# Turning q and k of the attention heads with VectorE and DMA instead of TensorE

## The chip, the cores and the metric

One Trainium2 chip, one core of it. The metric is the device time of one execution in microseconds (us), as a median over several runs; lower is better.

## The reference

One layer of a hybrid encoder over 512 tokens of width 1024, in float32. The normalised input is multiplied by one large matrix, whose columns feed an mLSTM branch (q, k, v, gates i, f, o, z; 4 heads of 256), a stick-breaking attention branch (q, k, v, z; 8 heads of 128) and the merge gates. What the change touches is the attention:

```
h = rmsnorm(x, norm_w);  proj = h @ w_in + b_in
qs = rmsnorm(to_heads(sq, 8), sb_q_norm_w);  ks = rmsnorm(to_heads(sk, 8), sb_k_norm_w)
# per block of 128 queries, for all keys up to its end:
z = (qb @ kb.T) * 128 ** -0.5
log_beta = log_sigmoid(z);  log_1mb = where(s < t, log_sigmoid(-z), 0)
between = reverse_cumsum(log_1mb) - log_1mb
out = where(s < t, exp(log_beta + between), 0) @ v
y_s = out * silu(sz)
...
q, k = silu(causal_depthwise_conv(mq | mk, width 4))        # mLSTM branch
merged = g_m * (y_m @ w_proj_m) + g_s * (y_s @ w_proj_s);  return x + merged @ w_out
```

## The kernel before

Every product is made of three matmuls: each operand is split into a high part (a copy rounded by ScalarE) and a low part (what is left, subtracted by VectorE), and high x high, high x low and low x high are added in PSUM (`mm3`, lines 85 to 87; `split`, lines 90 and 91). In the profile PE is TensorE, DVE VectorE, ACT ScalarE, POOL GpSimd and SP the engine that issues most DMAs.

The program is one list of 118 units, numbered c from 0. A unit is one block of weights and its 24 matmuls of 512 columns. Units 0 to 3 make q, 4 to 7 k, 8 to 11 v and 12 to 15 z of the first set of four attention heads (set 0); 16 to 19 q, 20 to 23 k, 24 to 27 z and 28 to 31 v of the second (set 1). The mLSTM pair 0 follows with o (32 to 35), z (36 to 39), v (40 to 43), q (44 to 47) and k (48 to 51), then pair 1, the gates, the two projections and the last products. The loop at the end of the program runs over the units. In unit c it evacuates unit c-1 from PSUM, splits the weights of unit c+2 (`ahead`; `wh` by ACT, line 90, `wl` by DVE, line 91; the loads on SP, `stg`, line 110, run up to four units ahead), issues the first 12 matmuls, lets each running attention or mLSTM head take one step, and issues the other 12. In the units listed in `REST` running heads take no step, but heads may start. Work that is due later is put off by `defer(n, ...)` to unit c+n, ahead of that unit's split.

A unit of a `tok_group` (q, k, v of the attention, v of the mLSTM) has tokens on the partitions and adds up a quarter of the sum in four banks of PSUM, all evacuated after the fourth. A unit of a `chan_group` has channels on the partitions and is evacuated by itself. The mLSTM's q and k are of that kind: the evacuation is the convolution (lines 646 to 667: a copy by ACT, `acc` in four operations on DVE, a sigmoid on ACT, a product on DVE, then the high part on ACT and the low part on DVE).

An attention head is a generator with a step per unit. Its start (lines 384 to 397) turns q and k of the head, which lie with tokens on partitions (`qraw`, `kraw`), by eight 128x128 transposes on TensorE (line 389) into PSUM and splits them there into `qth`, `qtl`, `kth`, `ktl`; q is scaled by `qkw` on the way. Then come the scores of three blocks and the weighing of two (two sigmoids on ACT, masks on POOL, a scan and a product on DVE, lines 408 to 423), the third block's scores, block transposes of the weights on DVE (line 440), 16 DMAs that finish their turning (line 458), the splits of the turned weights into `ath` and `atl` (lines 467 to 475), and the products with v (line 484), the last followed by the product with the gate into `ys` (line 493). `SB_START` and `M_START` give the first unit in which each head may start; it also waits for its set's k. Sixteen DMAs of 32 KB per mLSTM head turn its output in the same way (lines 780 and 801, `ht` and `hz`).

Of the kernel before, what the change touches and what calls it, by code (L numbers as in the profile page):

```python
# [17 lines left out]
TB = 4  # L18
# [5 lines left out]

SB_START = [10, 13, 16, 19, 26, 28, 31, 34]
M_START = [52, 56, 70, 76]
GATES_PREP, GATES_START = 3, 4
REST = {11, 16, 20, 23, 24, 32, 44, 64}  # L30
AHEAD, LOADS = 2, 4

# [2 lines left out]
def tile_hybrid_layer(  # L35
# [16 lines left out]
    nc = tc.nc  # L52
# [3 lines left out]
    def pool(name, bufs=1, **k):  # L56
# [4 lines left out]
    sp = pool("sp")  # L61
# [4 lines left out]
    ctx.enter_context(tc.manual_schedule())  # L66

    BUFS = {"stg": 3, "wh": 3, "wl": 3, "tmp": 2, "acc": 1, "om": 3, "P5": 2, "A": 4,
            "qk": 18, "vh": 5, "vl": 5, "y": 16, "brow": 1}

    MISC = {"om", "tmp", "acc", "brow", "stg"}

    def blk(tag, dt=F32, shape=(512,), name=None, p=128):

        where = mp if tag in MISC else sp
        return where.tile([p] + list(shape), dt, name=name or tag, tag=tag, bufs=BUFS[tag])

    def dense_ps():
# [111 lines left out]
    def defer(n, fn):  # L190
        later.setdefault(now[0] + n, []).append(fn)
# [19 lines left out]
    ident = cst.tile([128, 128], F32, name="ident")  # L211
# [6 lines left out]
    qkw = cst.tile([128, 1], F32, name="qkw")  # L218
# [91 lines left out]
    done = set()  # L310

    class SbSet:
        def __init__(self, s):
            self.s = s
            self.raw = {"q": [], "k": []}
            self.r = []
            self.v = []

        def z_group(self):
            def evac(ct, ps):  # L320
# [9 lines left out]
        def qk_group(self, name, c0):  # L330
            row = []

            def evac(tb, ps):
                t = blk("qk", name=name + "raw")
                nc.vector.tensor_tensor(t, ps, row[0], op=OP.add)
                self.raw[name].append(t)

                def norm():
                    ssq = tiny.tile([128, 4], F32, name="ssq", bufs=2)
                    rr = tiny.tile([128, 8], F32, name="r" + name, bufs=8 if name == "q" else 4)  # L340
                    r = rr[:, 0:4]
                    junk = blk("acc", BF, (128,), name="sqj")
                    for h in range(4):
                        nc.scalar.activation(junk, t[:, h * 128:(h + 1) * 128], AF.Square,
                                             accum_out=ssq[:, h:h + 1])
                    rstd(r, ssq, 128, EPS)
                    if name == "q":
# [35 lines left out]
        def head(self, h):  # L383
            hs = slice(h * 128, (h + 1) * 128)
            tr = []
            for name in ("q", "k"):
                tp = att_ps()
                for tb in range(TB):
                    nc.tensor.transpose(tp[:, tb * 128:(tb + 1) * 128], self.raw[name][tb][:, hs], ident)  # L389
                th = blk("qk", FR, name=name + "th")  # L390
                tl = blk("qk", FR, name=name + "tl")
                if name == "q":
# [4 lines left out]
                tr.append((th, tl))  # L397
# [218 lines left out]
    class MPair:  # L616
# [25 lines left out]
        def qk_group(self, name, c0, o):  # L642
            def evac(ct, ps):
                ch = o + 4 * self.p + ct
                t = blk("tmp")
                nc.scalar.activation(t, ps, AF.Identity, bias=bias(ch))
                self.prev()
                acc = blk("acc")
                nc.vector.tensor_scalar(acc, t, cw(3, ch), cb(ch), op0=OP.mult, op1=OP.add)
                for j in (1, 2, 3):  # L650
                    nc.vector.scalar_tensor_tensor(acc[:, j:], t[:, 0:T - j], cw(3 - j, ch), acc[:, j:],  # L651
                                                   op0=OP.mult, op1=OP.add)
                self.prev()
                nc.scalar.activation(t, acc, AF.Sigmoid)  # L654

                def mult():
                    nc.vector.scalar_tensor_tensor(t, acc, 1.0 if name == "q" else 0.0625, t,
                                                   op0=OP.mult, op1=OP.mult)

                    def high():  # L660
                        th = blk("qk", FR, name="m%sh" % name)
                        tl = blk("qk", FR, name="m%sl" % name)
                        nc.scalar.activation(th, t, AF.Copy)
                        self.tr[name].append((th, tl))

                        def low():
                            nc.vector.tensor_tensor(tl, t, th.bitcast(F32), op=OP.subtract)
# [12 lines left out]

            chan_group(w_in, c0 + 512 * self.p, 512, h_mov, evac, lambda: self.prev())
# [139 lines left out]
    for p in pairs:  # L821
        p.o_group()
        p.z_group()
        p.v_group()
        p.qk_group("q", C_MQ, 0)
        p.qk_group("k", C_MK, 8)

    gs_t, gm_t = [], []

    def gs_tile(ct):  # L830
        tag = ("brow", "om", "om", "acc", "qk")[min(ct, 4)]
        gs_t.append(blk(tag, shape=(516 if tag == "om" else 512,), name="gs")[:, 0:512])
        return gs_t[ct]

    def gm_tile(ct):
        gm_t.append(blk("qk", name="gm"))
        return gm_t[ct]

    def gate_group(c0, o, tile_of):
# [44 lines left out]
    chan_group(w_proj_s, 0, D, lambda k: ysp[k], ps_evac)  # L884

    merged = []

    def pm_evac(ct, ps):
# [4 lines left out]
        tl = blk("qk", FR, name="mgl")  # L893
# [196 lines left out]

    def first_split(i, low=None):
        u = units[i]
        for j in range(2):
            hi, lo = blk("qk", FR, name="fh"), blk("y", FR, name="fl")
            nc.scalar.activation(hi, u.st[:, j, :], AF.Copy)
            (low or nc.vector).tensor_tensor(lo, u.st[:, j, :], hi.bitcast(F32), op=OP.subtract)  # L1096
            f_w.append((hi, lo))
# [8 lines left out]
    nc.sync.dma_start(gst, w_in[:, C_MI:C_MI + 8].rearrange("(k p) c -> p k c", p=128))  # L1106
    load_vecs()

    idle = blk("qk", FR, name="idle")
    nc.vector.memset(idle.bitcast(F32), 0.0)  # L1110
    wp = dense_ps()

# [137 lines left out]
```

## Time and profile before

| | us |
|---|---|
| median of 3 runs (lowest, highest) | 700.15 (699.52, 700.24) |
| profiled execution, its own time | 700.42 |
| its span | 698.7 |
| TensorE busy | 690.4 |
| VectorE busy | 463.5 |
| ScalarE busy | 335.6 |
| GpSimd busy | 109.2 |

The times in the profile count from the start of the span; what lies around it, 700.42 - 698.7 = 1.7 us, is not in it. A row of a group gives the busy time, the mean duration in ns and the idle time just before; a row of the timeline gives the start, the duration and the instruction, with the idle time before it and what ended it in brackets. A matmul's duration is longer than the distance to the next, since they are pipelined: distances of starts are what counts.

### The profile page before, as it was taken

To read this page: it belongs to the slowest core of one execution; us is meant where nothing else is said; L and a number is where in the kernel's file an instruction comes from. 1 tells how busy PE (TensorE), PEld (TensorE's weight loads), DVE (VectorE), ACT (ScalarE), POOL (GpSimd) and SP (SyncE) were. 2 spreads that over 40 slices of the span, in tenths; PEclk is the share of its full clock that TensorE was granted. 3 is DMA by queue.
4 is the path that set the end of the run, shared out by engine and by line. 5 is a ranking of instruction groups with operands and counts; after the bars stand their busy time and mean duration, and the time that the engine had idled before them with its cause. 6 is when DMAs were issued, how large, how long until landed. Compare 5 with 4: busy or idle time off the path is not lost.

```text
span 698.7 us, 9267 instructions
## 1 busy us (share of the span) xinstructions
PE 690.4 (99%) x3220; PEld 575.2 (82%) x3220; DVE 463.5 (66%) x807; ACT 335.6 (48%) x629; POOL 109.2 (16%) x249
## 2 busy tenths in 40 slices
PE   7999999999999999999999999999999999999997
PEld 5888888888888888888888888888888888888876
DVE  6837887856787775389944738995343364445996
ACT  6245354475554543244475534446563353344451
POOL 5422122252130220000011120001111000111021
PEclk9999999999999999999999999999999999999999
DMA  7432424525433444333332244433323456589434
GB/s 247 136 106 71 126 63 123 148 59 145 112 107 84 130 109 137 90 95 94 97 98 67 61 108 120 120 90 91 91 61 86 112 157 219 144 184 208 126 81 130
DMA packets 104759, 80.94 MB, mean 116 GB/s; under 512 B 6766, under 2 KB 89096, under 8 KB 104712
## 3 DMA queue, kind: packets, MB, share of 16 engines
q1 hardware_dynamic: 102552, 74.45, 37.2%
q0 software_dynamic: 2016, 5.77, 4.5%
q8 instruction: 25, 0.41, 0.2%
q14 instruction: 22, 0.18, 0.1%
q10 hardware_dynamic: 144, 0.13, 0.1%
HBM read 65.12 MB, written 2.10 MB: 96 GB/s over the span
## 4 chain that ended last, share of the span: by engine, by line
PE 97%; DMA 1%; DVE 1%; POOL 0%; SPq 0%; issue 0%; ACT 0%; DVEq 0%
PE dps L85 27%; PE dps L86 27%; PE dps L87 27%; PE aps L86 3%; PE aps L87 3%; PE aps L85 3%; PE aps L389 1%; PE dps L1139 1%; PE dps L1137 1%; PE dps L1138 1%; DMA stg<-in_w_in_dram 1%; PE aps L760 1%; PE aps L762 1%; PE aps L761 1%; DVE fl L1096 0%; POOL fl L1096 0%
## 5 line engine op out<-in xcount | busy, mean ns | idle before, releaser
L91 DVE TENSOR_TENSOR wl<-stg,wh 128x1024 fp32r<-128x1024 f32 x92 | 112.6, 1223 | 112.9 <-ACT wh L90 111.3
L85 PE MATMUL dps<-hh,wh 128*128 128x512 f32 x448 | 175.2, 391 | 0.0
L87 PE MATMUL dps<-hh,wl 128*128 128x512 f32 x448 | 174.5, 389 | 0.0
L86 PE MATMUL dps<-hl,wh 128*128 128x512 f32 x448 | 174.5, 389 | 0.0
L90 ACT ACTIVATE wh<-stg 128x1024 fp32r<-128x1024 f32 x92 | 96.8, 1052 | 58.4 <-PE dps L87 38.2
L87 PEld LDWEIGHTS dps<-hh,wl 128*128 128x128 f32 x448 | 84.1, 188 | 17.8
L85 PEld LDWEIGHTS dps<-hh,wh 128*128 128x128 f32 x448 | 84.1, 188 | 17.1 <-DVE tmp L372 0.4
L86 PEld LDWEIGHTS dps<-hl,wh 128*128 128x128 f32 x448 | 84.2, 188 | 16.9
L85 PE MATMUL dps<-wh,hh 128*128 128x512 f32 x224 | 88.2, 394 | 0.1
L87 PE MATMUL dps<-wh,hl 128*128 128x512 f32 x224 | 87.3, 390 | 0.0
L86 PE MATMUL dps<-wl,hh 128*128 128x512 f32 x224 | 87.3, 390 | 0.0
L87 PEld LDWEIGHTS dps<-wh,hl 128*128 128x128 f32 x224 | 42.0, 188 | 9.0
L85 PEld LDWEIGHTS dps<-wh,hh 128*128 128x128 f32 x224 | 42.1, 188 | 8.6 <-issue 0.5
L86 PEld LDWEIGHTS dps<-wl,hh 128*128 128x128 f32 x224 | 42.1, 188 | 8.1
L651 DVE SCALAR_TENSOR_TENSOR acc<-tmp,vec,acc 128x511 f32<-128x511 f32 (+2 forms) x48 | 36.0, 750 | 1.7
L654 ACT ACTIVATE tmp<-acc 128x512 f32<-128x512 f32 x16 | 10.1, 633 | 50.8 <-DVE acc L651 50.8
L422 DVE TENSOR_TENSOR_SCAN om<-om 128x512 f32<-128x512 f32 (+3 forms) x32 | 26.7, 835 | 8.8 <-POOL om L416 8.8
L416 POOL TENSOR_SCALAR_AFFINE_SELECT om<-om 128x128 f32<-128x128 f32 x32 | 14.1, 441 | 109.0 <-ACT om L414 109.0
L713 POOL TENSOR_SCALAR_AFFINE_SELECT w_all<-om 128x128 f32<-128x128 f32 x16 | 6.0, 412 | 153.9 <-DVE om L708 136.8
L414 ACT ACTIVATE om<-aps,rq 128x512 f32<-128x512 f32 (+3 forms) x32 | 16.8, 525 | 22.8 <-PE aps L87 22.8
L85 PE MATMUL dps<-yh,wh 128*128 128x512 f32 x64 | 24.9, 389 | 0.0
L86 PE MATMUL dps<-yl,wh 128*128 128x512 f32 x64 | 24.9, 389 | 0.0
(271 smaller groups left out, 1225.3 us busy)
## 6 DMA issues: line engine op xcount, KB each, us to landing
stg<-in_w_in_dram SPq DMA_DIRECT2D x87, 512.0 KB, 3.8
az<-ay SPq DMA_DIRECT2D x128, 40.0 KB, 2.0
stg<-in_w_proj_s_dram SPq DMA_DIRECT2D x8, 512.0 KB, 3.7
B<-in_w_out_dram SPq DMA_DIRECT2D x8, 512.0 KB, 4.8
stg<-in_w_proj_m_dram SPq DMA_DIRECT2D x8, 512.0 KB, 3.6
wl<-stg POOLq DMA_DIRECT2D x8, 512.0 KB, 5.5
brow<-in_b_in_dram SPq DMA_DIRECT2D x8, 256.0 KB, 4.0
hz<-ht SPq DMA_DIRECT2D x64, 32.0 KB, 1.9
```

Source lines behind the costliest of these rows:

```text
L85: nc.tensor.matmul(ps, ah, bh, start=first, stop=False)
L86: nc.tensor.matmul(ps, ah, bl, start=False, stop=False)
L87: nc.tensor.matmul(ps, al, bh, start=False, stop=last)
L90: nc.scalar.activation(hi, src, AF.Copy)
L91: nc.vector.tensor_tensor(lo, src, hi.bitcast(F32), op=OP.subtract)
L389: nc.tensor.transpose(tp[:, tb * 128:(tb + 1) * 128], self.raw[name][tb][:, hs], ident)
L414: nc.scalar.activation(om[:, 0:n], zp, AF.Sigmoid, scale=rn[:, h:h + 1])
L416: nc.gpsimd.affine_select(out=om[:, ts], in_=om[:, ts], compare_op=OP.is_gt, fill=1.0, base=0, channel_multiplier=1, pattern=[[-1, 128]])
L422: nc.vector.tensor_tensor_scan(back, back, back, 1.0, op0=OP.mult, op1=OP.bypass)
L651: nc.vector.scalar_tensor_tensor(acc[:, j:], t[:, 0:T - j], cw(3 - j, ch), acc[:, j:], op0=OP.mult, op1=OP.add)
L654: nc.scalar.activation(t, acc, AF.Sigmoid)
L760: nc.tensor.matmul(nm[:, 0:258], ph, vh, start=j == 0, stop=False)
```

## The change

q of both sets and k of set 1 (the set `TURNED`) are no longer turned by TensorE. Per pair of heads, DVE transposes blocks of 32x32 in four operations of 128x256 (`turn`, line 387 ff. of the new kernel) into a buffer `ty`; one unit later 16 DMAs of 32 KB move the blocks to their places in `tz`, for set 0 all on SP, for set 1 half on SP and half on POOL. When a head starts, the q of its pair is scaled by `qkw` in one DVE operation on `tz` (128x1024, at the start of the pair's first head), and the high and low parts are made from `tz` in SBUF. k of set 0 is turned as before. The 18 buffers `qk` of 2 KB per partition become 9 of 4 KB that hold two tiles each.

The heads of set 1 may start at units 31, 33, 36 and 39 instead of 26, 28, 31 and 34. In pair 0 the v group moves behind q and k: q is now units 40 to 43, k 44 to 47, v 48 to 51.

```diff
-SB_START = [10, 13, 16, 19, 26, 28, 31, 34]
+SB_START = [10, 13, 16, 19, 31, 33, 36, 39]
+TURNED = {("q", 0), ("q", 1), ("k", 1)}
...
+                        if (name, self.s) in TURNED and tb == TB - 1:
+                            defer(1, lambda: self.turn(name, 0))
...
-                                done.add(("k", self.s))
+                                if (name, self.s) in TURNED:
+                                    self.turn(name, 0)
+                                else:
+                                    done.add(("k", self.s))
...
+        def turn(self, name, g):
+            ty = sp.tile([128, 8, TB, 32], F32, name="ty", tag="A", bufs=4)
+            for tb in range(TB):
+                nc.vector.transpose(ty[:, :, tb, :],
+                                    self.raw[name][tb][:, 256 * g:256 * g + 256].rearrange("p (x j) -> p x j", j=32))
+
+            def move():
+                tz = blk("qk", F32, (2, 4, 128), name="tz")
+                self.tz[name].append(tz)
+                src = ty.rearrange("p (h b) i j -> p b h (i j)", h=2)
+                for b in range(4):
+                    for a in range(4):
+                        q = nc.gpsimd if self.s and a % 2 else nc.sync
+                        q.dma_start(tz[32 * b:32 * b + 32, :, a, :], src[32 * a:32 * a + 32, b])
+
+            defer(1, move)
+            if g == 0:
+                defer(1 if name == "k" else 2, lambda: self.turn(name, 1))
+            elif name == "k":
+                defer(3, lambda: done.add(("k", self.s)))
...
-                tp = att_ps()
-                for tb in range(TB):
-                    nc.tensor.transpose(tp[:, tb * 128:(tb + 1) * 128], self.raw[name][tb][:, hs], ident)
...
+                if (name, self.s) in TURNED:
+                    tp = self.tz[name][h // 2][:, h % 2].rearrange("p a (i j) -> p i a j", j=32)
+                    th, tl = [x.rearrange("p (i a j) -> p i a j", a=4, j=32) for x in own]
+                    if name == "q" and h % 2 == 0:
+                        z = self.tz[name][h // 2]
+                        nc.vector.tensor_scalar(z, z, qkw, None, op0=OP.mult)
+                else:
+                    tp = att_ps()
+                    for tb in range(TB):
+                        nc.tensor.transpose(tp[:, tb * 128:(tb + 1) * 128], self.raw[name][tb][:, hs], ident)
...
-        p.v_group()
+        if p.p:
+            p.v_group()
         p.qk_group("q", C_MQ, 0)
         p.qk_group("k", C_MK, 8)
+        if not p.p:
+            p.v_group()
```

What stands in the engines' queues at the places that matter, first DVE in unit 31, ahead of the evacuation of v of set 1 (`tmp<-dps,brow`). Before:

```order
L91 TENSOR_TENSOR wl<-stg,wh 128x1024
L493 TENSOR_TENSOR ys<-aps,ys 128x512
L440 STREAM_TRANSPOSE ay<-a_all 128x4x32 x5
L394 SCALAR_TENSOR_TENSOR qtl<-aps,qkw,qth 128x512
L91 TENSOR_TENSOR ktl<-aps,kth 128x512
L372 TENSOR_TENSOR tmp<-dps,brow 128x512 x2
```

And after:

```order
L97 TENSOR_TENSOR wl<-stg,wh 128x1024
L540 TENSOR_TENSOR ys<-aps,ys 128x512
L434 TENSOR_SCALAR tz<-tz,qkw 128x1024
L97 TENSOR_TENSOR qtt<-tz,qtt 128x512
L97 TENSOR_TENSOR ktt<-tz,ktt 128x512
L413 TENSOR_TENSOR tmp<-dps,brow 128x512 x2
```

The block transposes of a running head are gone from here, since the heads start later, and the scaling of a pair's q has come in; q and k of the starting head are read from `tz`.

Second, DVE in the units 41 and 42, from one split of weights (`wl`) on. Before, with the v group of pair 0 in these units:

```order
L91 TENSOR_TENSOR wl<-stg,wh 128x1024
L493 TENSOR_TENSOR ys<-aps,ys 128x512
L91 TENSOR_TENSOR atl<-az,ath 128x512
L91 TENSOR_TENSOR atl<-az,ath 128x384
L91 TENSOR_TENSOR wl<-stg,wh 128x1024
L91 TENSOR_TENSOR atl<-az,ath 128x384
```

After, from the same split, all of it in unit 41:

```order
L97 TENSOR_TENSOR wl<-stg,wh 128x1024
L696 TENSOR_SCALAR acc<-tmp,vec 128x512
L698 SCALAR_TENSOR_TENSOR acc<-tmp,vec,acc 128x511
L698 SCALAR_TENSOR_TENSOR acc<-tmp,vec,acc 128x510
L698 SCALAR_TENSOR_TENSOR acc<-tmp,vec,acc 128x509
L540 TENSOR_TENSOR ys<-aps,ys 128x512
L97 TENSOR_TENSOR atl<-az,ath 128x384
L487 STREAM_TRANSPOSE ay<-a_all 128x4x32 x5
L469 SCALAR_TENSOR_TENSOR om<-om 128x256
L470 TENSOR_TENSOR a_all<-a_all,om 128x256
L469 SCALAR_TENSOR_TENSOR om<-om 128x384
L470 TENSOR_TENSOR a_all<-a_all,om 128x384
```

The convolution of pair 0's q (`acc`) now stands among the steps of the last heads of set 1.

Third, SP around the loads of the units 10 to 13 (`stg` is a block of weights, `brow` a row of biases). Before:

```order
L304 DMA brow<-in_b_in_dram 128x512
L110 DMA stg<-in_w_in_dram 128x2x512 x2
L110 DMA stg<-in_w_in_dram 128x8x128 x2
L304 DMA brow<-in_b_in_dram 128x512
L110 DMA stg<-in_w_in_dram 128x8x128 x2
```

And after:

```order
L310 DMA brow<-in_b_in_dram 128x512
L399 DMA tz<-ty 32x2x128 x16
L116 DMA stg<-in_w_in_dram 128x2x512 x2
L399 DMA tz<-ty 32x2x128 x16
L116 DMA stg<-in_w_in_dram 128x8x128 x2
L310 DMA brow<-in_b_in_dram 128x512
L116 DMA stg<-in_w_in_dram 128x8x128 x2
```

Two bursts of 16 transfers now stand ahead of these loads.

More of the change, by code (lines that the diff above doesn't have):

```diff
@@ L68, in tile_hybrid_layer @@
     BUFS = {"stg": 3, "wh": 3, "wl": 3, "tmp": 2, "acc": 1, "om": 3, "P5": 2, "A": 4,
-            "qk": 18, "vh": 5, "vl": 5, "y": 16, "brow": 1}
+            "qk": 9, "vh": 5, "vl": 5, "y": 16, "brow": 1}
     MISC = {"om", "tmp", "acc", "brow", "stg"}
@@ L76, in blk, with two @@
         return where.tile([p] + list(shape), dt, name=name or tag, tag=tag, bufs=BUFS[tag])
+    def two(tag, dt=F32, name=None):
+        t = blk(tag, dt, (2, 512), name=name)
+        return t[:, 0, :], t[:, 1, :]
     def dense_ps():
@@ L331, in qk_group @@
             row = []
+            half = []
             def evac(tb, ps):
-                t = blk("qk", name=name + "raw")
+                if tb % 2 == 0:
+                    half.extend(two("qk", name=name + "raw"))
+                t = half[tb]
                 nc.vector.tensor_tensor(t, ps, row[0], op=OP.add)
@@ L386, in head @@
             for name in ("q", "k"):
-                tp = att_ps()
-                for tb in range(TB):
[L389 to L392, printed above, removed]
+                th, tl = own = two("qk", FR, name=name + "tt")
+                if (name, self.s) in TURNED:
[8 more added lines that the diff above has]
+                        nc.tensor.transpose(tp[:, tb * 128:(tb + 1) * 128], self.raw[name][tb][:, hs], ident)
+                if name == "q" and not (name, self.s) in TURNED:
                     nc.scalar.activation(th, tp, AF.Copy, scale=qkw)
@@ L396, in head @@
                     split(tp, th, tl)
-                tr.append((th, tl))
+                tr.append(own)
             yield
@@ L660, in high @@
                     def high():
-                        th = blk("qk", FR, name="m%sh" % name)
-                        tl = blk("qk", FR, name="m%sl" % name)
+                        th, tl = two("qk", FR, name="m%st" % name)
                         nc.scalar.activation(th, t, AF.Copy)
@@ L823, in tile_hybrid_layer @@
         p.z_group()
-        p.v_group()
+        if p.p:
+            p.v_group()
         p.qk_group("q", C_MQ, 0)
         p.qk_group("k", C_MK, 8)
+        if not p.p:
+            p.v_group()
     gs_t, gm_t = [], []
     def gs_tile(ct):
-        tag = ("brow", "om", "om", "acc", "qk")[min(ct, 4)]
-        gs_t.append(blk(tag, shape=(516 if tag == "om" else 512,), name="gs")[:, 0:512])
+        if ct < 4:
+            tag = ("brow", "om", "om", "acc")[ct]
+            gs_t.append(blk(tag, shape=(516 if tag == "om" else 512,), name="gs")[:, 0:512])
+        elif ct % 2 == 0:
+            gs_t.extend(two("qk", name="gs"))
         return gs_t[ct]
     def gm_tile(ct):
-        gm_t.append(blk("qk", name="gm"))
+        if ct % 2 == 0:
+            gm_t.extend(two("qk", name="gm"))
         return gm_t[ct]
@@ L886, in tile_hybrid_layer @@
     merged = []
+    mgl = []
     def pm_evac(ct, ps):
@@ L892, in pm_evac @@
         th = blk("y", FR, name="mgh")
-        tl = blk("qk", FR, name="mgl")
+        if ct % 2 == 0:
+            mgl.extend(two("qk", FR, name="mgl"))
+        tl = mgl[ct]
         nc.scalar.activation(th, t, AF.Copy)
@@ L1092, in first_split @@
         u = units[i]
+        his = two("qk", FR, name="fh")
         for j in range(2):
-            hi, lo = blk("qk", FR, name="fh"), blk("y", FR, name="fl")
+            hi, lo = his[j], blk("y", FR, name="fl")
             nc.scalar.activation(hi, u.st[:, j, :], AF.Copy)
@@ L1107, in tile_hybrid_layer @@
     load_vecs()
-    idle = blk("qk", FR, name="idle")
+    idle = two("qk", FR, name="idle")[0]
     nc.vector.memset(idle.bitcast(F32), 0.0)
```

1 line of the change is left out of this document (added).

## The prediction

> **What bounds the kernel now.** I read the page first: the busy shares, the slices and the chain that ended last.
>
> ```profile
> PE 690.4 (99%) x3220; PEld 575.2 (82%) x3220; DVE 463.5 (66%) x807; ACT 335.6 (48%) x629; POOL 109.2 (16%) x249
> PEclk9999999999999999999999999999999999999999
> PE 97%; DMA 1%; DVE 1%; POOL 0%; SPq 0%; issue 0%; ACT 0%; DVEq 0%
> ```
>
> TensorE (PE) is busy 690.4 of 698.7 us at the full granted clock, and the chain is 97% PE. A microsecond of PE work that goes is a microsecond gained, as long as nothing that PE waits for becomes late. The other way round, VectorE (DVE), at 66%, costs nothing until it is late somewhere. The waits of PE name all there is now:
>
> ```profile
> PE dps L1115 <- DVE idle L1110: 1.5, 1, 1.5
> PE aps L293 <- DVE x L283: 1.0, 1, 1.0
> PE dps L1137 <- DVE hh L295: 0.9, 1, 0.9
> PE dps L1139 <- DVE fl L1096: 0.7, 1, 0.7
> ```
>
> All four lie in the start-up; behind it PE waits nowhere for long. So the question has two halves: how much PE work goes, and which of the producers that are just in time now come too late.
>
> **What goes from PE.** The head starts hold the transposes (groups of one line, then the timeline of PE around the start of the last head of the second set):
>
> ```profile
> L389 PE MATMUL aps<-ident,qraw x32: 270/272/328, 77.8 to 236.9; 128*128 128x128 f32 x32
> L389 PE MATMUL aps<-ident,kraw x32: 272/273/273, 78.3 to 237.3; 128*128 128x128 f32 x32
> 236.53 0.60 PE L389 MATMUL aps<-ident,qraw 128*128 128x128 f32 x4
> 236.96 0.60 PE L389 MATMUL aps<-ident,kraw 128*128 128x128 f32 x4
> 237.32 0.47 PE L85 MATMUL dps<-hh,wh 128*128 128x512 f32 x1
> 237.63 0.39 PE L86 MATMUL dps<-hl,wh 128*128 128x512 f32 x1
> 237.86 0.39 PE L87 MATMUL dps<-hh,wl 128*128 128x512 f32 x1
> ```
>
> A duration of 272 ns is not the price: they are pipelined. From start to start eight take 237.32 - 236.53 = 0.79 us, and the first matmul behind them takes a step of 0.31 instead of the 0.23 of the next one, so 0.87 for a head with q and k. The q of one head, four transposes, is half of it, 0.43. Removed are q and k for the four heads of the second set (4 x 0.87 = 3.5) and q of four heads of the first (4 x 0.43 = 1.7): 5.2 us of PE, 48 of the 64 transposes. The k of the first set stays.
>
> Here the Trainium skill speaks against the change: VectorE: DVE Perf Modes, Rules for kernel authors, sends a full 128x128 transpose to TensorE, and its section The three transpose paths prices it at 390 ns there and 311 ns on VectorE, which turns 32x32 blocks only. By that price the 48 would be worth 19 us on PE; the rows above, at 0.1 us a piece in the stream, decide, and since PE is the bound here I hold the move off it to be right in principle.
>
> **What comes to DVE.** Each pair of heads needs four block transposes of 128x256; this shape stands in the trace (another tile), and the scaling of a pair's q is an operation of 128x1024 like the one on x:
>
> ```profile
> L780 DVE STREAM_TRANSPOSE ht<-hns x16: 401/436/446, 393.4 to 551.5; 128x256 f32<-128x256 f32 x16
> L283 DVE TENSOR_SCALAR x<-x,xs x4: 753/760/1118, 6.2 to 20.6; 128x1024 f32<-128x1024 f32 x4
> ```
>
> 24 x 0.44 = 10.5 us and 4 x 0.76 = 3.0, together some 13 us on DVE (463 to 477), in six groups of 1.7 and four of 0.8. The low parts of q and k are still one operation each, from SBUF instead of PSUM; I cost that at nothing. By itself this lies beside PE: in the first set at units 5 and 7, in the second at 22 to 28, where weights are split more than one unit ahead.
>
> **The transfers.** 16 per pair and tensor of 32 KB, the same shape as the transfers of the later heads (timeline of SP, groups of POOL, list of DMA issues):
>
> ```profile
> 407.28 10.28 SPq L801 DMA_DIRECT2D hz<-ht  x16
> 417.66 0.53 SPq L110 DMA_DIRECT2D stg<-in_w_in_dram  x1
> L119 POOL DMA_DIRECT2D wl<-stg x8 | 7.1, 893 | 93.5 <-DVE yml L91 61.7 <-ACT wl L118 27.5 <-DVE B L938 4.3
> hz<-ht SPq DMA_DIRECT2D x64, 32.0 KB, 1.9
> stg<-in_w_in_dram SPq DMA_DIRECT2D x87, 512.0 KB, 3.8
> ```
>
> A burst holds SP for 10.3 us, and the next weight load waits behind it. In this row a load waited just so (417.66) without any wait of PE, since loads run four units ahead of use, 4 x 5.4 = 22 us, and a load needs 3.8. For the first set two such bursts lie in front of the loads of units 10 and 12; 10.3 us late plus 3.8 still fit in the lead. For the second set half goes through POOL: 8 issues x 0.9 = 7 us each, four times 7, so 29 us of POOL, which has 16% now. Behind them on POOL stand the scales of k (rstd) and later the masks of the heads; the last burst is issued in unit 28, three units or over 16 us ahead of the first head at unit 31, and two bursts need 14. I cost all this at nothing; the cover is the lead, and if it is gone each burst costs up to its 10 us less the lead left.
>
> **What becomes late: three places.** First, unit 20, whose PSUM banks are freed by the evacuation of q of the second set, and unit 32, freed by that of v:
>
> ```profile
> 138.34 1.87 DVE L335 TENSOR_TENSOR qraw<-dps,brow 128x512 f32<-128x512 f32 x3
> 139.16 0.47 PE L85 MATMUL dps<-wh,hh 128*128 128x512 f32 x1
> 217.31 0.69 DVE L493 TENSOR_TENSOR ys<-aps,ys 128x512 f32<-128x512 f32 x1 [1.04 <-PE aps L87]
> 217.92 1.08 DVE L440 STREAM_TRANSPOSE ay<-a_all 128x128 f32<-128x128 f32 x5
> 220.15 1.28 DVE L372 TENSOR_TENSOR tmp<-dps,brow 128x512 f32<-128x512 f32 x2
> 220.88 0.50 PE L85 MATMUL dps<-hh,wh 128*128 128x512 f32 x1
> ```
>
> Both are just in time already: the first evacuation ends at about 138.34 + 0.62 = 138.96 and PE starts at 139.16; 220.15 + 0.64 = 220.79 against 220.88. At unit 20 PE comes 0.43 earlier and DVE does the same as before in front of it: 0.4 stays as a wait. At unit 32 PE loses the transposes of the head started in unit 31 (0.87). DVE loses five block transposes (1.0), gets the scaling (0.7), and its chain from ys on is now ys 0.6, scaling 0.7, ScalarE's high part of q about 0.7, two low parts 1.2, so 217.31 + 3.2 = 220.5 instead of 220.15. PE could start at 220.8 - 0.87 = 219.9 and gets its bank at 221.2: 1.3 us of wait. Bounds 0.5 and 2.
>
> The third place is the large one. The q and k groups of the first mLSTM pair now run as units 40 to 47, under the last two attention heads of the second set, which start later. Their evacuation is the convolution, whose loop stands in the timeline of DVE:
>
> ```profile
> 328.48 1.23 DVE L91 TENSOR_TENSOR wl<-stg,wh 128x1024 fp32r<-128x1024 f32 x1 [0.26 <-ACT wh L90]
> 329.62 0.54 DVE L649 TENSOR_SCALAR acc<-tmp,vec 128x512 f32<-128x512 f32 x1
> 330.20 2.32 DVE L651 SCALAR_TENSOR_TENSOR acc<-tmp,vec,acc 128x511 f32<-128x511 f32 x3
> 332.43 0.69 DVE L667 TENSOR_TENSOR mql<-tmp,mqh 128x512 fp32r<-128x512 f32 x1
> 334.23 1.23 DVE L91 TENSOR_TENSOR wl<-stg,wh 128x1024 fp32r<-128x1024 f32 x1 [0.25 <-ACT wh L90]
> L422 DVE TENSOR_TENSOR_SCAN om<-om 128x512 f32<-128x512 f32 (+3 forms) x32 | 26.7, 835 | 8.8 <-POOL om L416 8.8
> L423 DVE TENSOR_TENSOR a_all<-a_all,om 128x512 f32<-128x512 f32 (+3 forms) x32 | 16.7, 523 | 3.5
> L91 DVE TENSOR_TENSOR atl<-az,ath 128x384 fp32r<-128x384 f32 (+1 forms) x24 | 13.9, 608 | 1.8 <-PE aps L86 1.4 <-ACT ath L90 0.3
> 281.23 1.23 DVE L91 TENSOR_TENSOR wl<-stg,wh 128x1024 fp32r<-128x1024 f32 x1 [3.53 <-ACT wh L90]
> ```
>
> The loop alone has a period of 334.23 - 328.48 = 5.75 us, and a unit of 24 matmuls takes PE 24 x 0.227 = 5.45. So DVE falls 0.3 us behind per unit even with no head beside it, and a head adds to a unit: two scans and two products 2 x (0.84 + 0.52) = 2.7, five transposes 1.0, the low parts atl of the attention weights 0.5 to 0.6 each, the product ys 0.6. I walk DVE from the split in unit 41 on, in us from PE's start of unit 41. Now that split comes 281.23, with 3.5 us idle ahead of it; after the change unit 40's masks lie there, and I put it at 1.7. Periods: unit 41 9.6 (split 1.15, convolution 2.8, ys 0.6, atl 0.5, transposes 1.0, two scans and products 2.7, the loop's last product 0.65, together 9.4, and 0.2 of waits for ScalarE and GpSimd), unit 42 6.8 (ys, transposes), 43 6.6 (two atl), 44 5.75, then in unit 45 5.2 until the last atl of the third head is there: 1.7 + 9.6 + 6.8 + 6.6 + 5.75 + 5.2 = 35.7. PE needs that operand in the middle of unit 46. Attention adds to PE's units by its columns at 0.227 us per 512: scores of three blocks or the first two products 2688 columns, 1.2; the rest 1152, 0.5. So PE is there at 7.7 + 6.0 + 5.45 + 5.45 + 6.6 + 2.7 = 33.9: it waits 1.8. By the same walk the first product of the fourth head, in unit 48, waits 1.1, and its last one not. Together 2.9, call it 3.0; a split at 1.0 and shorter waits inside unit 41 make it 1, and ScalarE being late with its halves (it shares each step) makes it 6.
>
> After unit 48 the v group has light evacuations and DVE catches up; the mLSTM heads start one unit earlier at most, which I cost at nothing.
>
> **Sum.** -5.2 + 0.4 + 1.3 + 3.0 = -0.5 us on the profiled execution of 700.42, whose span is 698.7: 699.9. The median of the runs shown, 700.15, lies 0.27 below the profiled one, so 699.6 as a median. The bounds: all waits at their low ends, -5.2 + 0.2 + 0.5 + 1 = -3.5; at their high ends, -5.2 + 0.6 + 2 + 6 = +3.4. A measurement of this kernel can tell about 0.2%, 1.4 us.
>
> **Rivals.**
> 1. The waits are hidden (34%): the walk overstates DVE, because its operations overlap more than the steps that I took, and the heads' operands come in time. For it: splits of weights run more than a unit ahead. Against: the margins at units 20 and 32 are a tenth of a microsecond now, and that is not an estimate. Time: 699.9 - 2 to - 4, about 696.8 as a median.
> 2. DVE's backlog under the convolution is larger than the gain (20%). Place: units 41 to 49. ScalarE waits for the convolution's sum before its sigmoid, and the split of the next weights and the heads' halves stand behind that; if each of three head steps there comes 1 us later than walked, the wait is 6 and not 3. It decides from 3.5 us of extra wait in all on. Time 700.15 - 0.5 + 3.5 = 703.1.
> 3. One of these waits grows past 3 us in one piece and PE's clock drops (4%). No row of before shows it, PE's longest wait there being 1.5 us: an estimate from the step, twice 0.227 us for some 15 matmuls, is +3.4 us, so 703 to 706. The rule is in the Trainium skill, TensorE: Matmul & The Clock Gate, Why this matters for your kernels: a pause of PE of over about 3 us brings half clock; the trace agrees only in that the pauses of up to 1.5 us left the clock at 9.
> 4. The transfers bite (6%): POOL's 8 issues take twice 0.9 us, the scales of k come 7 us later and the head at unit 31 waits a few us: 702.
>
> **How the numbers follow.** The forecast, 699.6 (gain and waits cancel within 1.4 us), has 36%. Faster by over 0.2%: rival 1, 34%. Slower: rivals 2, 3 and 4, 30%. The forecast's own range is 698.7 to 701.5; the range to hold 8 in 10 reaches to most of rival 1 and of rival 2: 696.2 to 703.3.
>
> **What would show it.** L389 falls to 16 transposes, and head starts of the second set to none on PE; DVE's busy time rises to about 477; PE's waits show new rows, for tmp or qraw evacuations at units 20 and 32 and for ath or atl around unit 46 and 48, of 0.4, 1.3 and 3 us. If there are none of the last, rival 1 holds. If the waits name tz, stg or rk, I have mispriced the transfers. If the PEclk row falls below 9 anywhere, it is rival 3.

## The result and the profile after

The changed kernel takes 707.82 us (median of 4 runs, 706.98 to 708.46) against 700.19 for the one before (4 runs). The ratio is 1.011, with a 95% interval of 1.0093 to 1.0128: 7.6 us slower. The prediction was 699.6 with a range up to 703.3. The page of the profiled execution (708.46 us, span 706.7) first, the busy shares, the granted clock and the chain that ended last:

```profile
PE 691.6 (98%) x3172; PEld 573.3 (81%) x3172; DVE 472.1 (67%) x835; ACT 335.1 (47%) x629; POOL 127.1 (18%) x281
PEclk9999999999999999989999999999999999999999
PE 87%; DVE 5%; issue 4%; DMA 1%; ACT 1%; SPq 1%; POOL 1%; DVEq 0%; ACTq 0%; POOLq 0%
```

48 matmuls are gone, and yet PE is busy 1.2 us longer: the digit 8 in the clock row says that it ran slower for a while. The chain was 97% PE and is 87% now, with 5% on VectorE and 4% in time for which the profile shows no reason (`issue`). The waits of PE say where (those of the start-up left out):

```profile
PE aps L91 <- ACT ath L96: 5.2, 2, 3.6
...
PE dps L91 <- DVE tmp L413: 1.2, 1, 1.2
...
PE dps L91 <- DVE qraw L346: 0.4, 1, 0.4
PE aps L92 <- DVE atl L97: 0.2, 1, 0.2
```

0.4 is the wait at unit 20 and 1.2 the one at unit 32, close to the 0.4 and 1.3 of the forecast. The 5.2 are two waits for the turned weights of a head (`ath`): 1.6 in unit 42, where I had none, and 3.6 in unit 46, where I had 1.8. What made them late stands in the timelines of ScalarE, VectorE and TensorE in units 40 and 41, each row with its idle time and what ended it:

```profile
267.12 1.20 ACT L96 ACTIVATE ath<-az 128x384 fp32r<-128x384 f32 x2 [1.53 <-PE aps L92]
275.27 0.52 ACT L96 ACTIVATE ath<-az 128x384 fp32r<-128x384 f32 x1 [6.95 <-PE aps L92]
275.70 0.67 ACT L461 ACTIVATE om<-aps,rq 128x512 f32<-128x512 f32 x1
```

```profile
267.94 1.16 DVE L97 TENSOR_TENSOR atl<-az,ath 128x384 fp32r<-128x384 f32 x2
275.82 0.56 DVE L97 TENSOR_TENSOR atl<-az,ath 128x384 fp32r<-128x384 f32 x1 [6.72 <-ACT ath L96]
...
279.64 1.22 DVE L97 TENSOR_TENSOR wl<-stg,wh 128x1024 fp32r<-128x1024 f32 x1
```

```profile
268.93 0.28 PE L93 MATMUL aps<-ktt,qtt 128*128 128x256 f32 x1
...
274.54 0.28 PE L91 MATMUL aps<-ath,vh 128*128 128x256 f32 x1
...
275.06 0.27 PE L93 MATMUL aps<-ath,vl 128*128 128x128 f32 x1
...
275.92 0.37 PE L91 MATMUL aps<-ath,vh 128*128 128x384 f32 x1
276.44 0.44 PE L92 MATMUL aps<-atl,vh 128*128 128x384 f32 x1
```

The third `ath` of unit 40, of the second head of set 1, does not wait for its data: it waits 6.95 us for a product of the first head, which PE reaches only in the middle of unit 41 (274.54 to 275.3). It needs a buffer that this product reads; the experiments below test this. `ath` and `atl` live in the 16 buffers `y`; eight hold the gates of the attention, four the first gates of the mLSTM, so four are left, and in unit 40 one head turns its last weights and the next its first, three pairs. ScalarE and VectorE take their work in order, so everything behind stands still for 6.9 us: the first two weighings of the fourth head, and the split of the weights, which comes at 279.64, 7.8 us behind PE's start of unit 41 (271.82). On top of this comes the convolution. The end of it, PE in unit 46:

```profile
310.50 0.39 PE L93 MATMUL dps<-hh,wl 128*128 128x512 f32 x1
314.50 0.58 PE L91 MATMUL aps<-ath,vh 128*128 128x256 f32 x1 [3.60 <-ACT ath L96]
...
317.18 0.63 PE L93 MATMUL dps<-hh,wl 128*128 128x512 f32 x1
317.60 0.63 PE L91 MATMUL dps<-hh,wh 128*128 128x512 f32 x1
...
321.00 0.39 PE L93 MATMUL dps<-hh,wl 128*128 128x512 f32 x1
321.23 0.40 PE L91 MATMUL dps<-hh,wh 128*128 128x512 f32 x1
```

Behind the wait the matmuls start 0.43 us apart instead of 0.23 until 321.0: half clock. The windows have the granted clock in the column PEclk (columns: PE, weight loads, DVE, ACT and POOL busy, PEclk, DMA share, GB/s):

```profile
318.00:321.00 3.00, 3.00 (x8) 2.31 (x7) 2.93 (x6) 0.64 (x1) 0.00 (x0) 0.50 0.52 169
321.00:324.00 3.00, 3.00 (x15) 2.48 (x14) 2.08 (x3) 2.15 (x3) 0.00 (x0) 1.00 0.00 0
```

The same happened behind the wait in unit 42, from 286.8 to 290.2. Comparing the starts of each unit in the two traces, the 8.0 us by which the span grew are: -0.2 start-up, -5.2 transposes, +0.4 unit 20, +1.4 unit 32, +2.1 and +4.1 the steps that hold the waits in units 42 and 46 (with the 0.4 by which `atl` comes behind `ath` each time), +1.6 and +3.1 the matmuls at half clock. That is 7.3. The other 0.7 is in unit 41. It lasts 8.6 us here and 7.9 us in e2 (below), where the third pair of turned weights is made in time. Here PE needs the low part of that pair in this unit, gets it only at 275.82 + 0.56, and goes on at 276.44 (the last row of PE above).

### The profile page after: what moved, and what is told of

Same layout as the page of the kernel before. It is cut to its first block, busy times and chain, and to the rows that moved or that the text cites. A ratio compares the mean times of both kernels' runs of the same rounds, so it can differ in the third digit from the quotient of the medians.

```text
span 706.7 us, 9367 instructions
## 1 busy us (share of the span) xinstructions
PE 691.6 (98%) x3172; PEld 573.3 (81%) x3172; DVE 472.1 (67%) x835; ACT 335.1 (47%) x629; POOL 127.1 (18%) x281
## 4 chain that ended last, share of the span: by engine, by line
PE 87%; DVE 5%; issue 4%; DMA 1%; ACT 1%; SPq 1%; POOL 1%; DVEq 0%; ACTq 0%; POOLq 0%
PE dps L91 24%; PE dps L92 24%; PE dps L93 24%; PE aps L92 3%; PE aps L93 3%; PE aps L91 3%; DVE acc L698 1%; PE dps L1196 1%; PE dps L1194 1%; PE dps L1195 1%; DMA stg<-in_w_in_dram 1%; PE aps L806 1%; PE aps L808 1%; PE aps L807 1%; SPq L505 1%
## 5 line engine op out<-in xcount | busy, mean ns | idle before, releaser
L463 POOL TENSOR_SCALAR_AFFINE_SELECT om<-om 128x128 f32<-128x128 f32 x32 | 15.7, 492 | 124.5 <-ACT om L461 124.3
L93 PE MATMUL dps<-yh,wl 128*128 128x512 f32 x64 | 24.9, 389 | 0.0
```

What stands on the lines that cost most here:

```text
L93: nc.tensor.matmul(ps, al, bh, start=False, stop=last)
L463: nc.gpsimd.affine_select(out=om[:, ts], in_=om[:, ts], compare_op=OP.is_gt, fill=1.0, base=0, channel_multiplier=1, pattern=[[-1, 128]])
```

## The experiments

Theory A: the new order makes two heads need six `y` buffers in unit 40, and the 7 us of standstill are what PE waits for in units 42 and 46. Theory B: VectorE is overloaded by the convolution beside two heads, whatever the buffers do. Rival E: the turning itself, VectorE's 13 us or the bursts, eats the gain. C and D are on the clock. All ratios are to the kernel before on the same chip, about 700.6 us there.

### The standstill: another start, another buffer

**e1_head_later**

```diff
-SB_START = [10, 13, 16, 19, 31, 33, 36, 39]
+SB_START = [10, 13, 16, 19, 31, 34, 36, 39]
```

> The changed kernel with one number changed: the second head of set 1 may start at unit 34 instead of 33, so that it does not turn its first weights in the same unit (40) in which the first head turns its last. Theory A (the cause is the shortage of y buffers in unit 40: an ath of the second head waits 6.9 us for the first head's last product in unit 41, and ScalarE and VectorE stand still behind it): the wait of 6.9 us goes, the split for unit 43 starts some 6 us earlier, the waits of PE in units 42 (1.6 us) and 46 (3.6 us) shrink to nothing and to 0 to 2 us, the clock stays at full speed, and the time is 697 to 700. Theory B (VectorE is simply overloaded by the convolution beside two heads, whatever the buffers do): the waits of PE stay about as they are, 705 to 709.

Measured: 701.51 us, ratio 1.0016 (1.0006 to 1.0025). The wait of 6.95 us is gone, as is the one in unit 42; in units 43 and 46 there are two of `ath`, together 1.6:

```profile
PE aps L91 <- ACT ath L96: 1.6, 2, 0.9
```

It missed A's range by 1.5 us and B's by 3.5. It is 0.9 us slower than before, so of the 5.2 that the transposes give nothing is left, and some 6 us are lost. Comparing the starts of its units with those of e13 (below), which waits nowhere but in unit 20, shows where: 1.4 at unit 32, 0.7 around unit 37, 1.4 in unit 43, 1.7 in unit 46, 0.7 in units 48 and 49, and 0.4 at unit 20 in both. So A's cause is borne out, but this start leaves waits under the convolution that A had not counted.

**e2_own_buffer**

```diff
-                ah, al = blk("y", FR, name="ath"), blk("y", FR, name="atl")
+                if self.s and h == 1 and js == (1,):
+                    ah, al = two("qk", FR, name="ath")
+                else:
+                    ah, al = blk("y", FR, name="ath"), blk("y", FR, name="atl")
```

> The changed kernel with the same order of everything, but the second head of set 1 takes the buffer for its second block of turned weights from the qk buffers instead of the y buffers. Theory A: the wait of the third ath in unit 40 for PE goes (6.9 us), PE's wait in unit 42 and the half clock behind it go (2.1 and 1.6 us), the one in unit 46 falls from 3.6 to about 1.5, too short for the clock to drop, one of about 1 in unit 48 may come: 698 to 700. Theory B: 705 to 709.

Measured: 699.76 us, ratio 0.9991 (0.9981 to 1.0000). One buffer of 4 KB per partition, for the high and the low part of this block, with the order of every engine's work unchanged, takes back the 8 us. The third `ath` now follows the other two at once (ScalarE), and the wait in unit 42 is gone; one of 1.1 us is left, in unit 46, and the clock did drop behind it, which A had excluded (waits of PE):

```profile
267.33 1.62 ACT L96 ACTIVATE ath<-az 128x384 fp32r<-128x384 f32 x3 [1.53 <-PE aps L92]
```

```profile
PE aps L91 <- ACT ath L96: 1.1, 1, 1.1
```

A holds, B falls as the cause of the 8 us.

### Which part of the change brings it

**e4_order_only**: the kernel before, with

```diff
-SB_START = [10, 13, 16, 19, 26, 28, 31, 34]
+SB_START = [10, 13, 16, 19, 31, 33, 36, 39]
...
-        p.v_group()
+        if p.p:
+            p.v_group()
         p.qk_group("q", C_MQ, 0)
         p.qk_group("k", C_MK, 8)
+        if not p.p:
+            p.v_group()
```

> The kernel before with the new order alone: the starts 31, 33, 36 and 39 for set 1 and the v group of pair 0 behind q and k; q and k are turned by TensorE as before. Theory A or B (the loss is in the new order): the waits of units 42 and 46 are there without any VectorE transposes or new DMAs, and the 5.2 us of transposes stay: 709 to 713. Rival E (the loss comes with the turning, by VectorE's 13 us, the bursts or the scaling): 699 to 702.

Measured: 711.47 us, ratio 1.0155 (1.0139 to 1.0172). Without any of the turning the same two waits are there, 1.6 and 4.9 us:

```profile
PE aps L85 <- ACT ath L90: 6.5, 2, 4.9
```

**e12_order_own_buffer**: e4 with the buffers of e2, here two `qk` buffers of the old size.

```diff
+                if self.s and h == 1 and js == (1,):
+                    ah, al = blk("qk", FR, name="ath"), blk("qk", FR, name="atl")
```

> As e4_order_only (the kernel before with the new order, q and k turned by TensorE), with the second head's second block of turned weights in qk buffers instead of y buffers. Theory A: as e2_own_buffer against the changed kernel, some 8 us come back of the 11 lost: 702 to 705. Rival: the buffer matters only together with the turning by VectorE; 710 to 712.

Measured: 703.36 us, ratio 1.0042 (1.0028 to 1.0055). 8 of the 11 us come back; the rest is the wait in unit 46 that is left in e2 too (1.1 us) and the slow matmuls behind it: by the starts of its units, all of the loss that is left lies in unit 46.

**e5_q_alone**: also with the v group of pair 0 ahead of q and k again.

```diff
-TURNED = {("q", 0), ("q", 1), ("k", 1)}
+TURNED = {("q", 0), ("q", 1)}
-SB_START = [10, 13, 16, 19, 31, 33, 36, 39]
+SB_START = [10, 13, 16, 19, 26, 28, 31, 34]
```

> The changed kernel with q alone turned by VectorE and DMA (both sets), k of set 1 by TensorE again, and with the starts 26, 28, 31, 34 and the v group of pair 0 where they were before. Theory A (the new order, with its lack of y buffers, is what cost 8 us; the turning by itself gains what goes from PE less the waits at units 20 and 32): 32 transposes go, 3.5 us; 0.4 comes back at unit 20 and about 1.2 at unit 32, where the scaling lies in VectorE's way: 1.9 us faster than before, about 698.5. Rival E (the turning itself eats its gain by VectorE's work and the bursts): 700 or more.

Measured: 700.53 us, ratio 0.9997 (0.9986 to 1.0009): no gain that can be told, 1.8 less than A expected, and by its time in the range of rival E. In its trace PE waits nowhere in units 40 to 49, so the order is what brought those waits; but ahead of unit 32 it waits longer than I put down, since in this order the five block transposes stay ahead of the scaling (PE's waits, then VectorE):

```profile
PE dps L91 <- DVE tmp L413: 1.8, 1, 1.8
```

```profile
216.54 1.07 DVE L487 STREAM_TRANSPOSE ay<-a_all 128x128 f32<-128x128 f32 x5
217.54 0.71 DVE L434 TENSOR_SCALAR tz<-tz,qkw 128x1024 f32<-128x1024 f32 x1
218.95 0.69 DVE L97 TENSOR_TENSOR qtt<-tz,qtt 128x512 fp32r<-128x512 f32 x1 [0.70 <-ACT qtt L96]
```

So E is right in part: with these starts the wait ahead of unit 32 takes half of the 3.5 us that the transposes give. From unit 4 to the last units 1.2 us of gain are left in the profiled execution; there the start-up took 0.8 us more than before and the last transfer of the kernel came 1.1 us later, which I take for variation between executions and have not tested.

**e8_q_set0_alone**: e5 with `TURNED = {("q", 0)}`.

> The changed kernel with q of set 0 alone turned by VectorE and DMA, and with the order of before: 16 transposes go, 1.7 us, and 0.4 comes back at unit 20: 1.3 us faster, 699.2. If the bursts of 10 us on SP ahead of the weights of units 10 and 12 delay PE, there is a wait for stg or wh in units 10 to 14 and less or nothing is gained: 700.5.

Measured: 699.51 us, ratio 0.9984 (0.9974 to 0.9993), 1.1 us faster for 1.3 expected. The bursts of SP in front of the weights of units 10 and 12 do not reach PE. They look alike in the changed kernel (timeline of SP):

```profile
45.95 10.80 SPq L399 DMA_DIRECT2D tz<-ty  x16
56.84 1.04 SPq L116 DMA_DIRECT2D stg<-in_w_in_dram  x2
60.01 10.22 SPq L399 DMA_DIRECT2D tz<-ty  x16
70.76 1.00 SPq L116 DMA_DIRECT2D stg<-in_w_in_dram  x2
```

### The clock

**e3_keep_clock**

```diff
             apply(0)
             apply(1)
             turn((2, 3))
             yield
+            if self.s and h in (1, 2):
+                wm = att_ps()
+                for _ in range((0, 6, 15)[h]):
+                    nc.tensor.matmul(wm, hh[:, 0, 0:128], hh[:, 0, :], start=True, stop=True)
             apply(2)
             apply(3)
```

> The changed kernel with matmuls whose result nothing reads put where PE waits: 6 ahead of the last products of the second head (unit 42), 15 ahead of those of the third (unit 46), 1.4 and 3.4 us of the 1.6 and 3.6 that PE waits there. Theory C (each of these waits makes the granted clock fall to a half for about 3.5 and 6.5 us, and that costs 1.6 and 3.5 us beside the waits): the same waits end at the same time, the clock stays at full speed, and the time falls by 4 to 5 us to about 703. Rival D (the clock falls for another reason, or its cost is hidden by VectorE's being late anyway): 707 to 708.5.

Measured: 708.29 us, ratio 1.0111 (1.0096 to 1.0126). **e10_after_again** and **e11_keep_clock_again** put both on one chip:

> The changed kernel once more, beside e11_keep_clock_again on the same chip: 707.5 to 708.5.

> e3_keep_clock once more. Its profile showed the clock at full speed and unit 54 begun 1.6 us earlier than in the changed kernel, but its times no gain. If the half clock costs anything, this is 1 to 2 us below e10_after_again; if not, within 0.7 us of it.

Measured: 708.08 (1.0105, 1.0090 to 1.0121) and 708.28 us (1.0109, 1.0095 to 1.0123). The clock did stay at full speed there (0.999 in the mean, 0.993 without), and C is still wrong in its size. In unit 42 the six matmuls had themselves to wait 1.2 us for a bank of PSUM, so PE still paused there. The wait in unit 46 ends when ScalarE and VectorE get there, whatever PE does (PE in e3, the 15 matmuls ahead):

```profile
310.02 3.56 PE L540 MATMUL aps<-hh 128*128 128x512 f32 x15
314.89 0.39 PE L91 MATMUL aps<-ath,vh 128*128 128x256 f32 x1 [1.31 <-ACT ath L96]
```

314.89, against 314.50 in the changed kernel, and the 0.4 between them is a later start-up: what the full clock saved behind unit 42 only made this wait longer. Behind unit 46 PE is 2.3 us earlier; another 0.7 is lost in units 48 and 49, where PE waits for `atl`, and unit 54 begins 1.6 us earlier in both profiles. The times do not show these 1.6. In both profiles the last accumulating transfer of the kernel (`xr`) landed so late that 1.1 and 1.3 us passed more than before between the last matmul and the end, and in that of e3 PE lost another 1.0 around unit 103, where it waits for a transfer of weights. The transfer at the end is as late in e5, which has none of these matmuls, so they need not be its cause; it stays open.

### What is left: the backlog of the convolution

**e6_scale_early**: e2, and the scaling of q out of VectorE's chain ahead of unit 32.

```diff
+            if name == "q" and self.s:
+                def scale_z():
+                    z = self.tz[name][g]
+                    nc.vector.tensor_scalar(z, z, qkw, None, op0=OP.mult)
+                defer(28 + 2 * g - now[0], scale_z)
...
-                    if name == "q" and h % 2 == 0:
+                    if name == "q" and h % 2 == 0 and not self.s:
```

> As e2_own_buffer, and the scaling of a pair's q of set 1 is done in units 28 and 30 instead of at the start of the pair's first head. If the wait ahead of unit 32 (1.2 us in the changed kernel) is VectorE's chain of ys, scaling, ScalarE's copy and two low parts, it falls to 0.5 or less, and the time by 0.7 to 0.9 against e2_own_buffer: about 699. If it is something else, nothing changes: 699.8.

Measured: 698.52 us, ratio 0.9971 (0.9959 to 0.9983). The wait ahead of unit 32 is gone, and 1.2 us with it.

**e7_pause**: e6 with 46 added to `REST`.

> As e6_scale_early, and running heads take no step in unit 46, so that the third head's last products come in unit 47. Theory A with VectorE's backlog behind the convolution as the rest of the loss: the wait of 1.1 us in unit 46 and the half clock of 3.4 us behind it (1.2 to 1.6 us) go, and the time falls to about 696.5, clearly below the kernel before. Rival: the wait moves with the step to unit 47 to 50, and the time stays at 698.5 to 699.5.

Measured: 698.80 us, ratio 0.9977 (0.9965 to 0.9989). The rival: the wait moved, to unit 48 (1.3, for the bank that the convolution has not emptied) and to the fourth head's products in unit 49 (0.3 and 0.2):

```profile
PE dps L91 <- ACT tmp L701: 1.3, 1, 1.3
...
PE aps L91 <- ACT ath L96: 0.3, 1, 0.3
PE aps L92 <- DVE atl L97: 0.2, 1, 0.2
```

**e9_low_on_gpsimd**: e6, and

```diff
-                            nc.vector.tensor_tensor(tl, t, th.bitcast(F32), op=OP.subtract)
+                            (nc.vector if self.p else nc.gpsimd).tensor_tensor(tl, t, th.bitcast(F32), op=OP.subtract)
```

> As e6_scale_early, and the low parts of pair 0's convolved q and k are subtracted on GpSimd instead of VectorE, 0.6 us of VectorE less in each of the units 42 to 49 (GpSimd needs 1.3 to 1.7 us for such a one and does nothing else there). If VectorE's backlog is what PE still waits for in units 46 and 48 (1.1 and 0.4 us, and a half clock between them), four of these, 2.4 us, come off it ahead of the third head's last products: the waits go, and the time is 695.5 to 697.5. If it is ScalarE's queue (the sigmoid that waits for the convolution's sum ahead of everything), the time stays at 698 to 699.

Measured: 704.72 us, ratio 1.0060 (1.0048 to 1.0073): slower by 6 us than e6. Timelines of GpSimd and VectorE at one unit, and the form of the VectorE operation over the kernel (min/median/max ns):

```profile
290.62 1.54 POOL L721 TENSOR_TENSOR mqt<-tmp,mqt 128x512 fp32r<-128x512 f32 x1 [5.55 <-ACT mqt L717]
```

```profile
290.92 1.52 DVE L704 TENSOR_SCALAR acc<-tmp,vec 128x512 f32<-128x512 f32 x1
292.48 2.32 DVE L706 SCALAR_TENSOR_TENSOR acc<-tmp,vec,acc 128x511 f32<-128x511 f32 x3
```

```profile
L704 DVE TENSOR_SCALAR acc<-tmp,vec x16: 540/543/1570, 273.9 to 476.8; 128x512 f32<-128x512 f32 x16
```

The first operation of the convolution took 1.50 to 1.57 us where it ran beside GpSimd's, in seven units, and 0.54 else: it ends 0.3 us behind GpSimd's each time. So 0.6 us less and 1.0 more on VectorE in each such unit, and ahead of the sigmoid. PE's wait in unit 46 became 4.5 us. That GpSimd and VectorE share an interface to SBUF stands in the Trainium skill, GPSIMD Engine Reference, Specifications; it names VectorE instructions in a two-port mode or with two SBUF inputs. The one that was held here has one such input; in which mode it ran the trace does not show. The run shows the price, 1.0 us an operation.

**e13_sigmoid_behind** with its comparison **e14_scale_early_again**:

```diff
-                nc.scalar.activation(t, acc, AF.Sigmoid)
+                sig = lambda: nc.scalar.activation(t, acc, AF.Sigmoid)
+                if self.p:
+                    sig()
+                else:
+                    behind.append(sig)
...
             for e in list(pend):
...
+        while behind:
+            behind.pop(0)()
         units[c].mm(1)
```

> As e6_scale_early, and for pair 0 the convolution's sigmoid, which waits for VectorE's sum, is issued behind the heads' step instead of ahead of it, so that ScalarE's halves of the turned weights (ath) do not wait for the sum. If the rest of the loss in units 46 to 48 (waits of 1.1 and 0.4 us, a half clock of 0.9) is ScalarE's order (sum, sigmoid, ath, then VectorE's atl), VectorE stands idle 0.7 to 0.9 us less per head step, the waits and the half clock go, and the time falls by 1.5 to 3 against e14: 695.5 to 697. If it is VectorE's own load, 698.5.

> e6_scale_early once more, for comparison on the same chip: 0.9971 of the kernel before, 698.2 to 698.8.

Measured: e13 695.63 us, ratio 0.9930 (0.9916 to 0.9943); e14 698.44 us, 0.9972 (0.9962 to 0.9983). Putting ScalarE's sigmoid, which waits for VectorE's sum, behind the head's copies instead of ahead of them takes all waits of units 42 to 49 away. ScalarE at the third head's last block, in e6 and then in e13 (`tmp<-acc` is the sigmoid):

```profile
305.46 0.63 ACT L709 ACTIVATE tmp<-acc 128x512 f32<-128x512 f32 x1 [3.07 <-DVE acc L706]
306.00 0.51 ACT L96 ACTIVATE ath<-az 128x384 fp32r<-128x384 f32 x1
```

```profile
300.48 0.51 ACT L96 ACTIVATE ath<-az 128x384 fp32r<-128x384 f32 x1
303.65 0.63 ACT L710 ACTIVATE tmp<-acc 128x512 f32<-128x512 f32 x1 [2.66 <-DVE acc L707]
```

These are all of PE's waits outside the start-up in e13:

```profile
PE dps L91 <- DVE qraw L347: 0.4, 1, 0.4
```

With the buffer, the early scaling and this order the change gains 5.0 us, the 5.2 of its transposes less the 0.4 of unit 20, within 0.2. The half clock that the expectations of e9 and e13 name was not there to be won: in the profile of e6 the granted clock is 1.00 from 300 to 332 us. A wait costs more than its row says: by the starts of the units, unit 46 is 1.9 us shorter in e13 than in e14, for waits of 1.1 and 0.2 at full clock.

## Why the prediction was wrong, point by point

- **What goes from PE**, 5.2 us: right. The unit starts show 0.87 less for a head with q and k, 0.41 to 0.44 for one with q.
- **VectorE's new work**, 13 us, and the transfers at nothing: right in the prices. The transposes took 409 and 417 ns, the scalings 739, which is 12.8 us in all; but VectorE's busy time rose by 8.6 us, to 472.1 and not to 477. The groups' busy times add up to 11.5, so neighbouring operations overlap, which the sum left out; the rest is not traced. GpSimd needed 4.2 to 4.5 us for 8 issues where I had 7, and no wait of PE names `tz`, `stg` or `rk`.
- **Units 20 and 32**: 0.4 and 1.3 forecast, 0.4 and 1.2 waited. e6 shows the second to be the scaling.
- **Unit 40 to 46, the step that failed**: "after the change unit 40's masks lie there, and I put it at 1.7". The split for unit 43 came 7.8 us behind the start of unit 41. The walk adds up durations and has no term for the buffers of the turned weights: the third pair of unit 40 waits for a product of unit 41. Without that wait the walk's end comes out: 314.5 minus the 6.1 that the split was late is 308.4, and e2 has PE go on at 307.7. That is partly luck. In e2 the split came 1.1 us behind the start of unit 41, earlier than the 1.7 of the walk, and VectorE stood idle for 1.8 us in all for ScalarE's `ath` (0.57, 0.68 and 0.57), where the walk has 0.2 for such waits. The 1.1 forecast for unit 48 did not come.
- **The other step that failed** is one that the prediction lacks: it nowhere counts how many steps the heads are apart. The starts 31 and 33 look as far apart as 26 and 28. But unit 32 is one of those without steps, so the head of unit 31 takes its second step in unit 33, and the two heads are one step apart instead of two. That is what puts three turnings into unit 40.
- **Rival 2**, a backlog larger than the gain, had the direction and the place, and 703.1 for 707.8. The 8 us came from the standstill, which it did not name. For what is left without that, e13 bears out its mechanism, ScalarE's halves queued behind the sigmoid that waits for the sum, and not VectorE's load: with the load unchanged the waits are gone.
- **Rival 3**, the clock (703 to 706), came true in its mechanism: one wait of 3.6 us, with a half clock behind it. But the clock also fell behind shorter pauses (below), and keeping it up gained nothing that the times show (e3, e10, e11).

## What to carry to other kernels

When heads or stages are shifted against each other, count the buffers of each ring in the new overlap, unit by unit, before the durations: a producer that waits for a buffer in an in-order queue takes everything behind it along, here 7 us on two engines for two buffers of 2 KB per partition. Count starts in steps that are really taken, rest units left out. And in an in-order queue put what waits for another engine behind what does not: the sigmoids of eight units, each moved behind the heads' copies, were worth 2.8 us.

## What the runs showed of the hardware that I had not expected

- The granted clock fell to a half behind pauses of PE of 1.6 + 0.2 us (unit 42; two waits with one matmul between them) and, in e2, 1.1 + 0.2 us, each time for 3.4 us (286.8 to 290.2 and 309.6 to 313.0), and behind 3.6 us for 6.7. It did not fall behind the same 1.6 + 0.2 in e4, nor behind the same 1.1 + 0.2 in e6 and e14, nor behind 1.8 us at unit 32 in e5. So the length of the pause alone does not decide. PE behind the wait of 1.58 us, in the changed kernel (0.43 us from start to start) and in e4 (0.23):

```profile
284.86 0.38 PE L91 MATMUL aps<-ath,vh 128*128 128x256 f32 x1 [1.58 <-ACT ath L96]
...
288.05 0.63 PE L91 MATMUL dps<-hh,wh 128*128 128x512 f32 x1
288.48 0.63 PE L92 MATMUL dps<-hl,wh 128*128 128x512 f32 x1
```

```profile
289.04 0.38 PE L85 MATMUL aps<-ath,vh 128*128 128x256 f32 x1 [1.58 <-ACT ath L90]
...
291.22 0.39 PE L86 MATMUL dps<-hl,wh 128*128 128x512 f32 x1
291.45 0.39 PE L87 MATMUL dps<-hh,wl 128*128 128x512 f32 x1
```

  The Trainium skill, TensorE: Matmul & The Clock Gate, What's actually happening, has a window of 3.4 us that runs freely; the stretches of half clock agree with that length, and two of these three pauses are shorter than the 3 us that the page names as the bound (Why this matters for your kernels).
- A VectorE operation with one input from SBUF took 1.52 instead of 0.54 us beside a GpSimd operation of 1.54 us, and ended 0.3 us behind it (e9).
- The start-up varies between executions: unit 4 began 0.2 us earlier to 1.7 us later than in the profile of before, in kernels that are alike up to there but for the buffers' names; differences below a microsecond are to be read from the stretch they belong to, not from one execution's time.
